# Another order of the second layer's W_in slices in a hybrid decoder trunk

## The chip, the cores and the metric

The kernel runs on one core of a Trainium2 chip. The metric is the device time of one execution in microseconds, lower is better; three runs are given by their median. Engines are named as in the profile: PE is TensorE (matmul; PEld its weight loads), DVE is VectorE, ACT is ScalarE, POOL is GpSimd, SP is the queue that issues the DMAs.

## The reference, cut to what matters

Two layers, 512 tokens, width 1024. One projection W_in feeds three mixers, whose outputs go through W_out; an MLP follows.

```python
for l in range(DEPTH):                                  # DEPTH = 2
    h = _rmsnorm(x, norm_mix_g[l])
    z = h @ w_in[l]
    q, k, v, qi, ki, wi, u5, z_ssd, xbc, dt_raw = _split(z, IN_SIZES)
    attn_out = _dsa_mixer(q, k, v, qi, ki, wi, ...)     # index scores, top-k of 128 keys, softmax, P x V
    s5_out = _s5_mixer(u5, ...)                         # complex state scan, gelu, gate
    ssd_out = _ssd_mixer(z_ssd, xbc, dt_raw, ...)       # conv, chunked scan, gate by z_ssd
    x = x + concatenate([attn_out, s5_out, ssd_out]) @ w_out[l]
    x = x + (relu(_rmsnorm(x, norm_mlp_g[l]) @ w_up[l]) ** 2) @ w_down[l]
```

In `_dsa_mixer` each query scores all earlier keys with 8 small index heads (`qi`, `ki`, `wi`); the 128 best keys alone take part in its attention.

## The kernel before

Products are in float32, each as three passes on high and low parts: `mm3` (L454 to L460) issues xh x whi, xl x whi and xh x wlo. x lies transposed (channels by tokens, 8 tiles), and a slice of W_in is taken in slabs of 128 or 256 rows. For the second layer the slabs were split earlier and lie in DRAM; `Slabs.load` (L167) fetches high and low parts, five buffers deep, in the order of the slices.

The slices of W_in (`W_SL`): `kv` (keys, index keys, values, index weights, dt), `qi` (index queries), `q` (queries), `xa` and `xb` (the two halves of the SSD inputs), `u5` (S5 input), `z` (the SSD gate). `trunk_in` goes through them in the order of `w_order`. kv, qi and q give token tiles (ACT copies them out of PSUM, L1219 to L1224); xa, xb, u5 and z give channel tiles (DVE multiplies them with the row factors `rb`: L1210, L1202, L1213). u5 goes through DRAM to a layout by channel group (L1205, L1207).

`mixers` runs nine generators side by side: `trunk_in`, `keys` (key rope and transposes, then the index scores of query blocks 1 to 3, L1071 to L1076), `select` (top-k: 16 rounds of MAX, L1086, and MATCH_REPLACE, L1087, for each block; the mask, L1090), `attention` (for the query blocks 0 to 3: split of the queries hhl, L1043, transposes, scores lg, softmax pe, pT, po, ml, L1133), `recurrent` for S5 and for SSD, and three of `out_proj`. `merge` takes the next step of the generator whose clock is lowest; the clocks advance by estimated costs times the `pace` of the plan, and `prio` shifts priorities. A scheduler then fixes each engine's order by these priorities, by what is ready and by buffers. PSUM has two groups of four banks, m and a; `bank` in the plan says which tile uses which (qi, q, xb, u5, z: m; xa, scores: a).

S5 (`s5`): s5v products from u5 (L709), ACT copies (L713 to L715), rotation and scan on DVE (L724 to L736, result X), s5y on PE (L748, L749), transposes (L760), gelu over DVE and ACT (`ge`, L762 to L766), glu products (L775), gate (`sig`, L777, L779), then high part `mh` on ACT (L784) and low part `ml` on DVE (L785). SSD (`ssd`): softplus of dt in 25 rows of 128x16 (L803 to L825, L332 to L352), conv (L844 to L858), four chunks (L869 to L920).

Of the kernel before, what the change touches and what calls it, by code (L numbers as in the profile page):

```python
# [69 lines left out]
        "bank": {"w_kv": "m", "w_qi": "m", "w_q": "m", "w_u5": "m", "w_xa": "a", "w_xb": "m", "w_z": "m", "kT": "a", "hT": "a", "ix": "a", "lg": "a", "pT": "m", "po": "a", "sB": "m", "sst": "a", "sU": "a", "sv": "m", "sy": "m", "st": "m", "sg": "a", "dds": "a", "dseg": "m", "darow": "m", "dT": "a", "ds": "a", "dy": "a", "dst": "a", "dn": "a", "db": "m"},  # L70
    },
    {
        "w_order": ("kv", "xa", "qi", "z", "u5", "q", "xb"),
        "top": ((1,), (2,), (3,)),
        "out": (("s5",), ("att",), ("ssd",)),
        "serial": "no",
# [1505 lines left out]
```

## Time and profile before

| | us |
|---|---|
| median of three runs | 1332.54 |
| the runs | 1331.55 to 1332.56 |
| the profiled execution, its own time | 1328.87 |
| its span | 1327.1 |
| PE busy | 1218.0 (92%) |
| DVE busy | 885.2 (67%) |
| ACT busy | 549.2 (41%) |

The mixers of the second layer lie between about 710 and 936 us of the span; ahead of them is the first layer, behind them the second layer's MLP, in both of which PE is nearly always busy. A busy PE is not a PE at its peak, since its records overlap and its clock has two levels, 1.2 and 2.4 GHz; PEclk is the part of the higher one that was granted.

### The profile page before, as it was taken

What the parts mean: (1) busy time and instruction counts of PE and PEld (TensorE: products, weight loads), DVE (VectorE), ACT (ScalarE), POOL (GpSimd) and SP (SyncE); (2) the same over time, 40 slices, a digit from 0 to 9 for tenths busy, and PEclk for the clock granted to TensorE, in tenths of its full rate; (3) what the DMA queues carried; (4) which work ended last, traced back from release to release, by engine and by line L of the source; (5) the groups of instructions that cost most, each with busy time, mean ns of one, the idle gap of its engine ahead of it and who ended that gap; (6) DMA issues with size and microseconds to landing.
All of it is one profiled execution on the core that took longest, in us unless ns stands there. A gap on an engine that the chain in (4) does not pass through costs nothing.

```text
span 1327.1 us, 17056 instructions
## 1 busy us (share of the span) xinstructions
PE 1218.0 (92%) x5708; PEld 977.1 (74%) x5708; DVE 885.2 (67%) x2024; ACT 549.2 (41%) x1128; POOL 169.7 (13%) x302
## 2 busy tenths in 40 slices
PE   5678957889999989999999989968999999999998
PEld 5566745458888868888888767754788888888887
DVE  5998999857886545665564699975475445444443
ACT  4245444664543533534443234455254233242331
POOL 2385100000796040000000000000000000000000
PEclk9889988899999999999999989978999999999999
DMA  5132220002567647677644634300323333333332
GB/s 189 40 88 70 74 74 24 9 1 72 148 213 257 214 146 252 224 262 230 227 149 137 219 120 124 120 17 1 111 88 97 101 97 96 96 96 99 100 110 81
DMA packets 139688, 161.64 MB, mean 122 GB/s; under 512 B 18768, under 2 KB 107600, under 8 KB 139600
## 3 DMA queue, kind: packets, MB, share of 16 engines
q1 hardware_dynamic: 139600, 160.55, 38.5%
q8 instruction: 45, 0.74, 0.2%
q14 instruction: 43, 0.35, 0.1%
HBM read 128.29 MB, written 31.03 MB: 120 GB/s over the span
## 4 chain that ended last, share of the span: by engine, by line
PE 62%; DVE 19%; issue 7%; POOL 6%; ACT 4%; DMA 1%; SPq 0%; ACTq 0%; DVEq 0%; POOLq 0%
PE pm L458 18%; PE pm L460 18%; PE pm L459 18%; PE po L1128 3%; DVE isc L1087 2%; DVE mx L1086 2%; DVE isc L1076 2%; PE pTp L1123 1%; DVE pe L1107 1%; DVE wlo L192 1%; DMA wraw<-in_w_in_dram 1%; POOL pt L660 1%; DVE cv L847 1%; ACT pe L1108 1%; POOL pt L661 1%
## 5 line engine op out<-in xcount | busy, mean ns | idle before, releaser
L192 DVE TENSOR_TENSOR wlo<-wraw,whi 128x512 fp32r<-128x512 f32 (+1 forms) x312 | 223.2, 718 | 243.0 <-ACT whi L191 241.4
L191 ACT ACTIVATE whi<-wraw 128x512 fp32r<-128x512 f32 (+1 forms) x312 | 194.1, 625 | 374.5 <-PE pm L459 236.9
L458 PE MATMUL pm<-xh,whi 128*128 128x512 f32 x640 | 252.4, 395 | 3.8 <-ACT q L1224 3.2
L460 PE MATMUL pm<-xh,wlo 128*128 128x512 f32 x640 | 250.1, 392 | 1.2 <-DVE wlo L192 1.2
L459 PE MATMUL pm<-xl,whi 128*128 128x512 f32 x640 | 250.9, 392 | 0.0
L460 PE MATMUL pm<-uh,wlo 128*128 128x512 f32 x512 | 199.7, 390 | 0.3 <-DVE wlo L192 0.3
L458 PE MATMUL pm<-uh,whi 128*128 128x512 f32 x512 | 199.6, 390 | 0.0
L459 PE MATMUL pm<-ul,whi 128*128 128x512 f32 x512 | 199.6, 390 | 0.0
L458 PEld LDWEIGHTS pm<-xh,whi 128*128 128x128 f32 x640 | 120.8, 189 | 30.8 <-ACT q L1224 3.9
L460 PEld LDWEIGHTS pm<-xh,wlo 128*128 128x128 f32 x640 | 120.6, 189 | 27.4 <-DVE wlo L192 2.0
L459 PEld LDWEIGHTS pm<-xl,whi 128*128 128x128 f32 x640 | 121.1, 189 | 24.2 <-issue 0.2
L460 PEld LDWEIGHTS pm<-uh,wlo 128*128 128x128 f32 x512 | 96.2, 188 | 20.8 <-DVE wlo L192 0.9
L459 PEld LDWEIGHTS pm<-ul,whi 128*128 128x128 f32 x512 | 96.3, 188 | 20.4 <-issue 0.4
L458 PEld LDWEIGHTS pm<-uh,whi 128*128 128x128 f32 x512 | 96.2, 188 | 20.3 <-issue 0.4
L458 PE MATMUL pm<-whi,xh 128*128 128x512 f32 (+1 forms) x176 | 67.4, 385 | 14.0 <-ACT xh L392 12.8
L460 PE MATMUL pm<-whi,xl 128*128 128x512 f32 (+1 forms) x176 | 66.6, 380 | 1.3 <-DVE xl L394 1.3
L459 PE MATMUL pm<-wlo,xh 128*128 128x512 f32 (+1 forms) x176 | 67.0, 381 | 0.5 <-DVE wlo L192 0.3
L1408 DVE TENSOR_TENSOR ul<-ur,uh 128x512 fp32r<-128x512 f32 x64 | 48.5, 758 | 21.0 <-ACT uh L1407 21.0
L1406 DVE SCALAR_TENSOR_TENSOR ur<-pm,ur 128x512 f32<-128x512 f32 x64 | 43.9, 686 | 23.0 <-ACT ur L1403 22.7
L1414 DVE TENSOR_TENSOR sq<-pm,r2b 128x512 f32<-128x512 f32 x64 | 44.1, 689 | 17.5 <-PE pm L460 17.5
L1407 ACT ACTIVATE uh<-ur 128x512 fp32r<-128x512 f32 x64 | 39.9, 624 | 30.7 <-DVE ur L1406 30.7
L1087 DVE MATCH_REPLACE8 isc<-mx,isc 128x256 f32<-128x256 f32 (+2 forms) x96 | 51.6, 541 | 0.0
(345 smaller groups left out, 1931.4 us busy)
## 6 DMA issues: line engine op xcount, KB each, us to landing
wraw<-in_w_up_dram SPq DMA_DIRECT2D x128, 256.0 KB, 2.8
wraw<-in_w_down_dram SPq DMA_DIRECT2D x128, 256.0 KB, 2.8
st<-shi SPq DMA_DIRECT2D x48, 256.0 KB, 2.9
st<-slo SPq DMA_DIRECT2D x48, 256.0 KB, 3.5
wlo<-st SPq DMA_DIRECT2D x48, 256.0 KB, 3.0
whi<-st SPq DMA_DIRECT2D x48, 256.0 KB, 2.8
wraw<-in_w_in_dram SPq DMA_DIRECT2D x32, 256.0 KB, 2.8
sraw<-in_w_in_dram SPq DMA_DIRECT2D x32, 256.0 KB, 3.9
```

The lines of the kernel that those rows point to most:

```text
L191: nc.scalar.activation(hi, raw, AF.Copy)
L192: nc.vector.tensor_tensor(lo, raw, hi.bitcast(F32), ALU.subtract)
L458: nc.tensor.matmul(p, lh, rh, start=first, stop=False)
L459: nc.tensor.matmul(p, lh, rl, start=False, stop=False)
L460: nc.tensor.matmul(p, ll, rh, start=False, stop=last)
L1076: v.scalar_tensor_tensor(acc, r, wi[:, h:h + 1], acc, ALU.mult, ALU.add)
L1087: v.match_replace(acc, m8, acc, SENT)
L1128: nc.tensor.matmul(po[g_ * 64:g_ * 64 + 64], self.vt[:, kb, g_], pts[g_], start=kb == 0, stop=kb == b)
L1406: v.scalar_tensor_tensor(r, p, 0.0, r, ALU.max, ALU.mult)
L1407: nc.scalar.activation(h, r, AF.Copy)
L1408: v.tensor_tensor(lo, r, h.bitcast(F32), ALU.subtract)
L1414: v.tensor_tensor(t, d[1], rb, ALU.mult)
```

## The change

One line of the plan of the second layer: the order of the W_in slices.

```diff
 PLAN = (
...
     {
-        "w_order": ("kv", "xa", "qi", "z", "u5", "q", "xb"),
+        "w_order": ("kv", "qi", "q", "xa", "xb", "u5", "z"),
         "top": ((1,), (2,), (3,)),
         "out": (("s5",), ("att",), ("ssd",)),
```

The line sets the order of the slabs on SP and of the products on PE, and through `merge` and the scheduler the places of all that depends on them. Three places of the DVE queue show it.

The first is right behind the key work of the second layer (klo: low part of the keys; xa, scr, cv: SSD input, softplus and conv; qi, rsw: index queries and their rope; isc: index scores). Before:

```order
L1026 TENSOR_TENSOR klo_7429<-ksb_7148,khi_7427 128x384
L1210 TENSOR_TENSOR xa_7497<-pm_7321,rb_7490 128x512
L344 TENSOR_SCALAR scr_7506<-spe_7502 128x16
L1210 TENSOR_TENSOR xa_7555<-pm_7441,rb_7490 128x512
L345 TENSOR_SCALAR scr_7506<-scr_7506 128x16
L844 TENSOR_SCALAR cv_7635<-xa_7497,hconvw,hconvb 128x512
L346 TENSOR_SCALAR scr_7506<-scr_7506 128x16
L847 SCALAR_TENSOR_TENSOR cv_7635<-xa_7497,hconvw,cv_7635 128x511
```

The change:

```order
L1026 TENSOR_TENSOR klo_7426<-ksb_7148,khi_7424 128x384
L1002 TENSOR_TENSOR rsw_7533<-qi_7531,cols 128x8x8
L1003 TENSOR_TENSOR rsw_7533<-qi_7531,cols 128x8x8
L1004 TENSOR_TENSOR qi_7531<-qi_7531,cols 128x8x16
L1005 TENSOR_TENSOR qi_7531<-qi_7531,rsw_7533 128x8x16
L1043 TENSOR_TENSOR hhl_7538<-qi_7531,hhl_7538 128x4x64
L1043 TENSOR_TENSOR hhl_7548<-qi_7531,hhl_7548 128x4x64
L1073 TENSOR_SCALAR isc_7558<-irl_7562,wd_7150 128x256
```

The two xa tiles, the softplus and the conv behind the keys are gone from here; the index queries follow at once.

The second is S5 from its last X to its last ml (mx and isc: top-k; ge, sig, ml: S5). Before, from ge on:

```order
L764 TENSOR_TENSOR ge_8231<-ge_8231,s5yT_8226 128x512
L1087 MATCH_REPLACE isc_7773<-mx_2429_8988,isc_7773 128x384
L766 SCALAR_TENSOR_TENSOR ge_8220<-ge_8220,s5yT_8215 128x512
L766 SCALAR_TENSOR_TENSOR ge_8231<-ge_8231,s5yT_8226 128x512
L1086 MAX mx_2430_8991<-isc_7773 128x8
L1087 MATCH_REPLACE isc_7853<-mx_2500_9237,isc_7853 128x512
L1087 MATCH_REPLACE isc_7773<-mx_2430_8991,isc_7773 128x384
L1086 MAX mx_2501_9240<-isc_7853 128x8
L1086 MAX mx_2434_9011<-isc_7773 128x8
L779 SCALAR_TENSOR_TENSOR sig_8244<-sig_8244,ge_8220 128x256
L779 SCALAR_TENSOR_TENSOR sig_8244<-sig_8244,ge_8231 128x256
L1087 MATCH_REPLACE isc_7773<-mx_2434_9011,isc_7773 128x384
```

The change, from X on:

```order
L735 TENSOR_TENSOR sws_8613<-sws_8613,SIN_4941 128x512
L736 TENSOR_TENSOR X_2343_8580<-sw_8604,sws_8613 128x8x63
L763 TENSOR_SCALAR ge_8664<-ge_8664 128x512
L764 TENSOR_TENSOR ge_8664<-ge_8664,s5yT_8659 128x512
L763 TENSOR_SCALAR ge_8675<-ge_8675 128x512
L764 TENSOR_TENSOR ge_8675<-ge_8675,s5yT_8670 128x512
L766 SCALAR_TENSOR_TENSOR ge_8664<-ge_8664,s5yT_8659 128x512
L766 SCALAR_TENSOR_TENSOR ge_8675<-ge_8675,s5yT_8670 128x512
L779 SCALAR_TENSOR_TENSOR sig_8688<-sig_8688,ge_8664 128x256
L779 SCALAR_TENSOR_TENSOR sig_8688<-sig_8688,ge_8675 128x256
L785 SCALAR_TENSOR_TENSOR ml_8693<-sig_8688,mh_8692 128x512
```

Before, top-k rows of blocks 2 and 3 (isc 128x384 and 128x512) stand between S5's rows; now the last top-k row stands ahead of S5 and S5's rows follow each other.

The third is the first split of query block 2, hhl (gm, dec, xd, yss: SSD chunk 0; x: out products of S5 added to x; CT, cv: conv; z: the gate). Before:

```order
L844 TENSOR_SCALAR cv_8864<-xb_8862,hconvw,hconvb 128x512
L847 SCALAR_TENSOR_TENSOR cv_8864<-xb_8862,hconvw,cv_8864 128x511
L847 SCALAR_TENSOR_TENSOR cv_8864<-xb_8862,hconvw,cv_8864 128x510
L847 SCALAR_TENSOR_TENSOR cv_8864<-xb_8862,hconvw,cv_8864 128x509
L857 MEMSET CT_8871 64x512
L857 MEMSET CT_8872 64x512
L858 SCALAR_TENSOR_TENSOR CT_8871<-cth_8869,cv_8864 64x512
L1043 TENSOR_TENSOR hhl_8909<-q_8414,hhl_8909 128x4x64
L858 SCALAR_TENSOR_TENSOR CT_8872<-cth_8869,cv_8864 64x512
L894 TENSOR_TENSOR gm_8938<-ssds_8939,cons 128x256
L1043 TENSOR_TENSOR hhl_8919<-q_8414,hhl_8919 128x4x64
L896 TENSOR_TENSOR dec_8890<-dec_8890,gm_8938 128x512
```

The change:

```order
L1213 SCALAR_TENSOR_TENSOR z_8875<-pm_8722,rb_8172 128x512
L1133 TENSOR_TENSOR ml_7936<-po_8439,mh_7932 128x128
L1373 TENSOR_TENSOR x_103<-x_103,pm_8821 128x512
L1133 TENSOR_TENSOR ml_7937<-po_8439,mh_7933 128x128
L1373 TENSOR_TENSOR x_107<-x_107,pm_8833 128x512
L1133 TENSOR_TENSOR ml_7938<-po_8439,mh_7934 128x128
L1373 TENSOR_TENSOR x_113<-x_113,pm_8841 128x512
L1373 TENSOR_TENSOR x_117<-x_117,pm_8853 128x512
L894 TENSOR_TENSOR gm_8938<-ssds_8939,cons 128x256
L1043 TENSOR_TENSOR hhl_8909<-q_7892,hhl_8909 128x4x64
L896 TENSOR_TENSOR dec_8890<-dec_8890,gm_8938 128x512
L1043 TENSOR_TENSOR hhl_8919<-q_7892,hhl_8919 128x4x64
```

Before, the split follows the conv of xb; now the adds of S5's out products and z's tiles stand ahead of it. Behind it the rows are the same but for one add of x.

## Rows read from the trace of the kernel before

**Rows 1.** The page's slices: busy tenths of PE and DVE in 40 equal parts of the span.

```profile
PE   5678957889999989999999989968999999999998
...
DVE  5998999857886545665564699975475445444443
```

**Rows 2.** Stage windows: from:to, us; busy us of each engine (instructions); PEclk; DMA share, GB/s.

```profile
712.00:880.40 168.40, 145.98 (x728) 114.42 (x726) 140.72 (x446) 68.83 (x179) 0.53 (x1) 0.94 0.39 125
790.00:840.00 50.00, 44.34 (x241) 36.44 (x242) 49.78 (x151) 20.66 (x45) 0.53 (x1) 0.90 0.43 130
```

**Rows 3.** Timeline of DVE: start, us, engine, line, operation, output<-inputs, [idle before <-releaser].

```profile
733.05 0.69 DVE L1210 TENSOR_TENSOR xa<-pm,rb 128x512 f32<-128x512 f32 x1 [6.71 <-ACT rb L1192]
...
747.49 0.23 DVE L1002 TENSOR_TENSOR rsw<-qi,cols 128x64 f32<-128x64 f32 x1 [4.35 <-ACT qi L1224]
```

**Rows 4.** Timeline of PE behind the key slices: first xa, first qi, first key transpose.

```profile
710.97 0.39 PE L458 MATMUL pm<-xh,whi 128*128 128x512 f32 x1
...
716.43 0.39 PE L458 MATMUL pm<-whi,xh 128*128 128x512 f32 x1
...
721.51 0.90 PE L1030 MATMUL kTp<-cons,khi 128*128 128x128 f32 x3 [2.88 <-ACT khi L1024]
```

**Rows 5.** Timeline of ACT: first PSUM block of kv emptied, first index queries copied.

```profile
712.69 0.27 ACT L1221 ACTIVATE wd<-pm,rstd 128x12 f32<-128x12 f32 x1
...
746.77 0.69 ACT L1224 ACTIVATE qi<-pm,rstd 128x512 f32<-128x512 f32 x1 [3.05 <-PE pm L460]
```

**Rows 6.** Timeline of DVE ahead of the last attention blocks; 880.38 is block 2's first split.

```profile
851.98 0.29 DVE L1133 TENSOR_TENSOR ml<-po,mh 128x128 fp32r<-128x128 f32 x1 [0.71 <-ACT mh L1132]
...
872.26 0.29 DVE L1133 TENSOR_TENSOR ml<-po,mh 128x128 fp32r<-128x128 f32 x1 [2.91 <-ACT mh L1132]
...
872.47 0.74 DVE L847 SCALAR_TENSOR_TENSOR cv<-xb,hconvw,cv 128x510 f32<-128x510 f32 x1
...
880.38 0.42 DVE L1043 TENSOR_TENSOR hhl<-q,hhl 128x256 fp32r<-128x256 f32 x1
```

**Rows 7.** Timeline of DVE: a small chain alone, and a small row between others.

```profile
740.61 1.23 DVE L816 SCALAR_TENSOR_TENSOR spq<-spq,sps 128x16 f32<-128x16 f32 x6
...
837.02 0.17 DVE L326 SCALAR_TENSOR_TENSOR rst<-rst,qms 128x32 f32<-128x32 f32 x1
...
837.12 0.41 DVE L1043 TENSOR_TENSOR hhl<-q,hhl 128x256 fp32r<-128x256 f32 x1
```

**Rows 8.** Timelines of DVE, PE and ACT: u5, s5v, then pT and po of block 0.

```profile
785.97 1.12 DVE L1202 TENSOR_TENSOR u<-pm,rb 128x512 f32<-128x512 f32 x1
...
792.26 3.76 PE L709 MATMUL s5v<-U,BPT 128*128 128x128 f32 x16 [5.24 <-DVE isc L1087]
...
849.74 0.60 ACT L1125 ACTIVATE pT<-pTp 128x512 f32<-128x512 f32 x1 [1.98 <-PE pTp L1123]
...
850.56 1.07 PE L1128 MATMUL po<-pT,vt 128*64 128x512 f32 x2
```

**Rows 9.** Timeline of DVE: S5 from its last X to its first ml.

```profile
811.10 0.66 DVE L736 TENSOR_TENSOR X<-sw,sws 128x504 f32<-128x504 f32 x1
...
817.24 0.90 DVE L763 TENSOR_SCALAR ge<-ge 128x512 f32<-128x512 f32 x2
...
818.05 1.28 DVE L764 TENSOR_TENSOR ge<-ge,s5yT 128x512 f32<-128x512 f32 x2
...
819.78 1.27 DVE L766 SCALAR_TENSOR_TENSOR ge<-ge,s5yT 128x512 f32<-128x512 f32 x2
...
823.68 0.74 DVE L779 SCALAR_TENSOR_TENSOR sig<-sig,ge 128x256 f32<-128x256 f32 x2
...
825.69 1.08 DVE L785 SCALAR_TENSOR_TENSOR ml<-sig,mh 128x512 fp32r<-128x512 f32 x1
```

**Rows 10.** Windows of PE's granted clock behind waits; columns as in rows 2.

```profile
792.00:796.00 4.00, 3.73 (x17) 3.54 (x17) 4.00 (x12) 1.14 (x3) 0.53 (x1) 0.50 0.59 170
...
884.00:888.00 4.00, 4.00 (x20) 3.38 (x19) 1.95 (x6) 2.29 (x7) 0.00 (x0) 0.50 0.00 0
```

## The prediction

> **What bounds the kernel now.** I read the page's slices first: behind the opening, VectorE (DVE) has its only stretch of nines a little past the middle of the span, and just there TensorE (PE) has its one dip, 9968 [rows 1]. The stage windows say why [rows 2]: from 712 us, when the second layer's row factors are ready, to 880.4 us, DVE is busy 140.72 of 168.40 us, and from 790 to 840 it is busy 49.78 of 50. PE is busy 145.98 of the same 168.40, but in part it waits inside this for DVE. So this stage ends when DVE has got through its queue, and since an engine takes its queue in order, the stage costs the DVE work plus the DVE waits. The work is the same in both kernels (same formulas, same shapes). I forecast the change in the waits.
>
> I measure at one instruction, **E**: the first split (L1043) of query block 2, at 880.38 [rows 6]. From E on both kernels have nearly the same rows on PE, DVE and ACT (blocks 2 and 3 of the attention, the SSD chunks), so a later E is a later end. 168.40 - 140.72 = 27.7 us before E is not busy on DVE; the waits that follow are parts of it.
>
> **The change part by part.** The table moves the slices; PLAN's paces stay. No instruction is added or dropped; what moves are W_in's slabs (their loads on SP too), the products on them and all that hangs on these.
>
> (a) *Index queries first.* Now PE does 48 products for xa from 710.97 on, and DVE waits 6.71 us for ACT's rb and 4.35 us for the first index queries [rows 3]; ACT's copy of the first of them, from 746.77, lets DVE go [rows 5]. One product takes (716.43 - 710.97) / 24 = 0.2275 us. Without xa's 48 products (10.9 us), the rb broadcast and the stop at sds, that copy comes some 15 us sooner, at about 731. The banks cost nothing net: qi needs PSUM bank m, which ACT empties from 712.96 on [rows 5], so PE stands still for 2 us, but it stood still for 2.88 us at 721.51 in any case, for khi [rows 4]. DVE reaches its first index row at about 732 instead of 747.49. But the 10 us of xa, conv and softplus work that it did meanwhile are only put off. What counts is the wait: 11.06 us of it become 5.8 (from 733.05 - 6.71 = 726.3, the end of the key work, to 732). **-5.5** (bounds -4 and -6.5).
>
> (b) The waits of 2.91 and 0.71 us for ACT's copies of attention output [rows 6], and three of 0.15 to 0.29 beside them for out products, lose their place: **-4.3**.
>
> (c) The softplus chain of SSD (some 25 rows of 128x16) stood alone, 6 rows in 1.23 us, 0.205 each; a small row that stands between independent ones takes the queue for 0.10 (837.02 to 837.12) [rows 7]. In the new order the chain alternates with top-k and conv rows: about 25 x 0.1, **-2.4** (bounds 0 and -3). The Trainium skill's page Perfetto Trace Analysis (section Per-instruction lifecycle) says that each DVE instruction pays a fixed bubble for its memory latency; with that alone the order would not matter and this term would be 0. The rows show otherwise, and I take the rows.
>
> (d) The first attention block comes before xa on PE. Its second PSUM result reaches DVE about 1.4 us late instead of 0.7: **+0.7**, within the bounds of (e).
>
> (e) *The last three heads of index block 3.* Their scores now stand on PE between products for xa, behind the transpose of query block 1, which waits for DVE's split. From that split to the eighth head: 30 products (6.8 us), three score pairs and a transpose (1.8), ACT's relu (0.7), 9.3 us. DVE has twelve top-k and mask rows of about half a microsecond to do meanwhile, 6.2 us, so it waits 3.1. PE has just stood still for 2 to 3 us there, and after such stops the rows show 1.2 GHz: granted clock 0.50 in 792 to 796, behind a wait of 5.24 us [rows 8, 10]. Nine or ten of the 30 products at twice 0.2275 add 2.2: **+5** (bounds 2 and 8). Only behind this can top-k of block 3 begin.
>
> (f) *S5's input.* u5 is now taken off PSUM late, and from there to the first s5v it was 5.2 us (787.09 to 792.26, through DRAM on SP) [rows 8]. This trip lies beside top-k rows and block 1 of the attention. But the fourth s5v stands on PE behind block 1's P x V, which needs rows that DVE normalises last. From these rows on: pT 0.6 and po 1.07 [rows 8], s5v 0.9 (a quarter of 3.76), ACT's six small copies, for which I put 2, and 1 us of hand-overs, against some 2 us of DVE work: **+3.5** (bounds 1 and 5).
>
> (g) *The cover of S5 is gone.* This is the largest term. Before, S5's DVE rows stood among top-k rows of blocks 2 and 3, and its hops over PE and ACT were filled. In the new order top-k is finished (its last row stands just ahead of the first sv), and DVE has from sv to ml nothing but S5; what follows stands behind it in the queue. Each hop becomes a DVE wait, of the length that the trace shows [rows 9]: last X ends at 811.76, first ge row at 817.24: 5.5 (s5y, two copies, transposes, square). ge to ge over ACT's tanh: I put 0.6 (it was 0.45, with a top-k row in it: 819.33 to 819.78). Last ge row ends at 821.05, sig at 823.68: 2.6 (glu, tanh). sig's end at 824.42 to ml at 825.69: 1.2 (mh on ACT), twice. Sum **+11.1** (bounds 9 and 12.5). In the trace of before none of these shows as a wait of DVE: the windows have it busy 49.78 of 50 us there [rows 2].
>
> (h) *The out products of S5* then stand between ml and E on PE: 48 products, 10.9 us, with po, arow, ssdT and ssds among them; z's two tiles and two more share bank m, so x2 to x6 also wait for DVE adds. From ml's end to E I count 13.7 us, DVE's own rows there 12.0: **+1.7** (bounds 0 and 3).
>
> (i) *Clock.* During the hops of (g) PE stands still for 2 to 5 us at a time. By the granted clock of 0.50 after such stops [rows 10], I give s5y +1.7, glu +1.8 and the out products +1.5: **+5** (bounds 1 and 9).
>
> (j) *Behind E.* Before, PE came to E out of a nearly idle stretch and had granted clock 0.50 until 888 [rows 10]; now it comes out of the out products. **-1.5** (bounds 0 and -3).
>
> Sum: -5.5 - 4.3 - 2.4 + 0.7 + 5 + 3.5 + 11.1 + 1.7 + 5 - 1.5 = **+13.3**; walked through in order of time, engine by engine with the same durations, so that PE's stops pile up, I come to +16. I take the middle, +14.5. The profiled execution took 1328.87 with a span of 1327.1; its span becomes 1341.6. The median of the runs is 3.7 above that execution, so I add to the median: 1332.5 + 14.5 = **1347.0**, 1.1% more. All bounds low give -3, all high +30.
>
> **Rivals.**
>
> *The filled engine (faster).* DVE stays full from the first index row to E, as it does from 790 to 840 now [rows 2]: its rows start some 15 us sooner, the last waits go, and S5 finds something to run beside. Then only (a) to (c) count: 1332.5 - 12.2 = 1320.3. For it: top-k is the long chain, and it does start sooner. Against it: nothing stands beside S5 in the DVE queue, and an engine that waits at the head of its queue doesn't go past, as in the 2.91 us with conv rows (872.47 the first) ready behind it [rows 6]. It decides if S5's hops cost under 2 us in all. Chance 0.08. The Trainium skill's Perfetto Trace Analysis (section Engine Utilization) says that in a well-optimized kernel at least one engine should come near full use; read as a rule for this stage, it is this rival, and the rows from 790 to 840 fit it, while the new order doesn't.
>
> *PE early (no change).* (e), (f), (h) and (i) come to nothing, because PE keeps 2.4 GHz and waits less: -12.2 + 0.7 + 11.1 - 1.5 = -1.9, 1330.6. Against it: PE waits for DVE's splits in (e) whatever its clock. Chance 0.08.
>
> *PE slow (slower still).* PE's stops keep it at 1.2 GHz through S5 and the whole out block: 48 products at 0.43 (about twice 0.2275) instead of 0.2275 add 10 us to (h), of which (i) has 1.5. 1347 + 8.5 = 1355.5, with (e) at its upper end 1358.5. For it: granted clock 0.50 as late as 884 to 888, behind a stretch in which PE was nearly idle [rows 10]. Chance 0.15.
>
> **How the numbers follow.** Forecast (1337 to 1353): 0.69; PE slow 0.15; no change 0.08; filled engine 0.08. Range 1337 to 1358: it leaves out the two rivals below and the end of the one above. A measurement of this kernel can't tell less than 0.2% (2.7 us) from no change; slower by more 0.84, within 0.08, faster by more 0.08.
>
> **What the profile of the changed kernel would show.** DVE's first L1002 on qi near 732. Waits on DVE before the last two L1076 of block 3 (2 to 3 us each). L763 with a wait of 5 to 7 us for ACT's ge, L779 with 2.5 to 4.5 for ACT's sig, both L785 with about 1.2 for mh. E at 893 to 899 rather than 880.38. In this stretch PE with granted clock 0.5 to 0.8. I am wrong if these waits are there but E isn't later (then DVE work shrank), or if they are short (then S5's hops were not what the rows of before show), or if E is later by this and the end is not (then the tail had slack).

## The result, and the profile after

The changed kernel takes **1350.84 us** (median of four runs, 1347.38 to 1353.67) against 1332.05 for the kernel before in the same comparison: a ratio of 1.0146, 95% interval 1.0132 to 1.016, or 18.8 us more. The forecast was 1347.0 with a range of 1337 to 1358.

The profiled execution of the changed kernel took 1353.67 us with a span of 1351.9, 24.8 more than the span before. 3.6 us of that arise ahead of the second layer's mixers, in code that is the same in both: the row factors' first DVE row (L420) starts at 713.28 instead of 709.68. In the profiles of the twelve experiments below it starts between 710.9 and 714.2, so it is the profiled execution of before that was early. I therefore measure from this row, **M**, to E. M to E was 880.38 - 709.68 = 170.7 us, and is 904.68 - 713.28 = 191.4: **+20.7**. From E to the span's end it was 446.7 and is 447.2. The profiled execution of the changed kernel is the slowest of its four, which is one reason why 20.7 is more than 18.8.

The page's slices of the changed kernel; they answer to [rows 1]:

```profile
PE   5778967889999989999999887787999999999998
...
DVE  5998999757787535565654979576475444445443
```

The one dip of PE (9968) has become six slices (887787), and DVE has lost its run of nines. Stage windows of the changed kernel, columns as in [rows 2]:

```profile
715.60:904.70 189.10, 155.67 (x733) 120.88 (x733) 142.31 (x447) 69.41 (x179) 0.53 (x1) 0.91 0.34 108
...
867.00:877.00 10.00, 6.39 (x54) 6.06 (x55) 1.97 (x3) 2.34 (x6) 0.00 (x0) 0.55 0.01 4
...
881.00:887.00 6.00, 5.86 (x15) 4.78 (x16) 1.49 (x4) 1.29 (x3) 0.00 (x0) 0.56 0.00 0
888.00:900.00 12.00, 9.92 (x40) 6.08 (x39) 10.45 (x18) 3.44 (x7) 0.00 (x0) 1.00 0.27 87
```

The stage is 20.7 us longer, DVE's busy time 142.3 instead of 140.7: the loss is waiting. The two stretches in the middle lie in S5's hops, the times in which S5's chain is on PE and ACT and DVE has to wait for it: DVE and ACT are mostly idle there, and PE has little more than half its clock (granted 0.55 and 0.56). The waits, from DVE's timeline of the changed kernel (start, us, engine, line, operation, tiles, [idle before <-releaser]):

```profile
736.11 0.23 DVE L1002 TENSOR_TENSOR rsw<-qi,cols 128x64 f32<-128x64 f32 x1 [7.10 <-ACT qi L1224]
...
792.13 0.29 DVE L1133 TENSOR_TENSOR ml<-po,mh 128x128 fp32r<-128x128 f32 x1 [1.72 <-ACT mh L1132]
...
804.48 0.75 DVE L1076 SCALAR_TENSOR_TENSOR isc<-irl,wd,isc 128x512 f32<-128x512 f32 x1 [1.26 <-ACT irl L1071]
807.66 0.75 DVE L1076 SCALAR_TENSOR_TENSOR isc<-irl,wd,isc 128x512 f32<-128x512 f32 x1 [2.42 <-ACT irl L1071]
...
856.82 0.69 DVE L724 TENSOR_TENSOR sv<-sv,COS 128x512 f32<-128x512 f32 x1 [3.63 <-ACT sv L713]
...
868.07 0.69 DVE L734 TENSOR_TENSOR sw<-sw,COS 128x512 f32<-128x512 f32 x1 [1.39 <-ACT sws L733]
...
878.10 0.43 DVE L763 TENSOR_SCALAR ge<-ge 128x512 f32<-128x512 f32 x1 [8.02 <-ACT ge L762]
...
885.65 0.76 DVE L779 SCALAR_TENSOR_TENSOR sig<-sig,ge 128x256 f32<-128x256 f32 x2 [3.82 <-ACT sig L777]
887.63 1.06 DVE L785 SCALAR_TENSOR_TENSOR ml<-sig,mh 128x512 fp32r<-128x512 f32 x1 [1.22 <-ACT mh L784]
...
890.58 1.06 DVE L785 SCALAR_TENSOR_TENSOR ml<-sig,mh 128x512 fp32r<-128x512 f32 x1 [1.22 <-ACT mh L784]
...
904.68 0.43 DVE L1043 TENSOR_TENSOR hhl<-q,hhl 128x256 fp32r<-128x256 f32 x1
```

S5's four waits alone are 8.02 + 3.82 + 1.22 + 1.22 = 14.28 us where [rows 9] show none. The last row is E.

**One sum for all kernels.** For each kernel of the table I add up the brackets of DVE's timeline between M and E ("waits") and call the rest of that stretch the rows' own time; of this the top-k rows (L1086, L1087), each counted from its start to the next row's start (less that row's bracket), stand apart. "Same" counts, in DVE's order, top-k rows that stand right behind a row of their own block, of 96.

| kernel | M to E | waits | rows | top-k | same | median less before |
|---|---|---|---|---|---|---|
| before | 170.7 | 24.8 | 145.9 | 49.2 | 11 | 0 |
| changed | 191.4 | 44.0 | 147.4 | 52.4 | 33 | +18.8 |
| e1 index queries first | 179.9 | 31.1 | 148.8 | 53.0 | 40 | +8.3 |
| e2 u5 last | 187.5 | 40.2 | 147.3 | 50.2 | 18 | +16.7 |
| e3 changed, longer hops | 198.3 | 50.8 | 147.5 | 52.4 | 33 | +25.8 |
| e4 before, longer hops | 176.3 | 30.0 | 146.3 | 49.3 | 15 | +4.9 |
| e5 changed, PE kept busy | 193.4 | 46.0 | 147.4 | 52.4 | 33 | +20.8 |
| e6 changed, s5y by halves | 187.2 | 39.8 | 147.4 | 52.3 | 33 | +18.7 |
| e7 before, s5y by halves | 172.9 | 27.1 | 145.8 | 49.6 | 15 | +1.6 |
| e8 q, then u5 | 180.4 | 30.3 | 150.1 | 54.1 | 44 | +10.7 |
| e9 q early, S5 covered | 172.7 | 26.0 | 146.7 | 50.0 | 20 | -0.2 |
| e10 u5 in front | 185.5 | 42.9 | 142.6 | (some behind E) | 10 | +14.1 |
| e11 top-k of 2 and 3 as one | 171.0 | 25.6 | 145.5 | 49.4 | 9 | +2.9 |
| e12 xb early | 169.1 | 22.8 | 146.3 | 49.5 | 15 | -1.3 |

M to E less 170.7 gives the difference of the medians to within 2.2 us in every row but e11, where it is 2.6: 20.7 for 18.8, 9.2 for 8.3, 16.8 for 16.7, 2.0 for -0.2. The medians come from other executions than the profile, and part of the agreement is luck: the profile of e1 is the fastest of its five executions and needs 442.0 us behind E instead of 446.7, and that of e6 is the fastest of its four.

### The profile page after: what moved, and what is told of

Its sections match the earlier page's. It is cut to its first block, busy times and chain, and to the rows that moved or that the text cites. A ratio compares the mean times of both kernels' runs of the same rounds, so it can differ in the third digit from the quotient of the medians.

```text
span 1351.9 us, 17050 instructions
## 1 busy us (share of the span) xinstructions
PE 1230.7 (91%) x5708; PEld 983.1 (73%) x5708; DVE 886.5 (66%) x2024; ACT 550.0 (41%) x1128; POOL 170.2 (13%) x302
## 4 chain that ended last, share of the span: by engine, by line
PE 72%; DVE 18%; ACT 4%; issue 2%; DMA 2%; POOL 1%; SPq 0%; ACTq 0%; DVEq 0%
PE pm L458 21%; PE pm L460 21%; PE pm L459 21%; PE po L1128 3%; DVE isc L1087 2%; DVE mx L1086 2%; PE pTp L1123 1%; DVE pe L1107 1%; DVE wlo L192 1%; DMA wraw<-in_w_in_dram 1%; DVE isc L1076 1%; DVE cv L847 1%; ACT pe L1108 1%; PE hTp L1046 1%; PE glu L775 1%
## 5 line engine op out<-in xcount | busy, mean ns | idle before, releaser
L458 PE MATMUL pm<-mh,whi 128*128 128x512 f32 x128 | 51.2, 403 | 1.5 <-DVE x L1373 0.6
```

The lines of the kernel that those rows point to most:

```text
L458: nc.tensor.matmul(p, lh, rh, start=first, stop=False)
```

## The experiments

Two theories stood at the start. **Theory 1:** the loss is S5's hops, which have no other DVE rows between them. **Theory 2:** the loss comes from index queries and queries being moved ahead of xa. The first two runs each make one half of the change.

### Each half alone: e1 and e2

```diff
-        "w_order": ("kv", "xa", "qi", "z", "u5", "q", "xb"),
+        "w_order": ("kv", "qi", "xa", "z", "u5", "q", "xb"),
```

> Order kv, qi, xa, z, u5, q, xb: the index queries go first, as in the changed kernel, but S5's input stays where it was, ahead of the queries, and S5's DVE rows keep top-k rows between them (8 rows between the last X and the first L763, 3 ahead of the first L779). Theory 1 (the loss of the change is S5's hops without cover on DVE): the wait before the first L1002 is about 7 instead of 11 us in all (-4), the waits before L763 and L779 stay under 2 us, top-k loses some interleaving (+2): 1329 to 1333 us. Theory 2 (the loss comes from moving the index queries ahead: the top-k rounds then run one block after the other): 1340 us or more, without a long wait in S5.

```diff
-        "w_order": ("kv", "xa", "qi", "z", "u5", "q", "xb"),
+        "w_order": ("kv", "xa", "qi", "z", "q", "xb", "u5"),
```

> Order kv, xa, qi, z, q, xb, u5: the order of before, with S5's input moved to the end alone; no row stands between S5's rows from the last X to the last ml. Theory 1: S5's hops turn into DVE waits (L763 some 8 us, L779 3.8, L785 1.2 twice, sv 3 to 4), less what the lost waits for mh give back (-3 to -4): 1342 to 1350 us. Theory 2 (the loss comes from index queries and queries ahead of xa): 1330 to 1335 us.

e2 took 1348.62 us (ratio 1.0126, 1.0111 to 1.0141): u5's place alone costs 16.7 us, where the whole change costs 18.8. DVE's timeline of e2:

```profile
879.07 0.43 DVE L763 TENSOR_SCALAR ge<-ge 128x512 f32<-128x512 f32 x1 [6.89 <-ACT ge L762]
...
886.14 0.43 DVE L779 SCALAR_TENSOR_TENSOR sig<-sig,ge 128x256 f32<-128x256 f32 x1 [3.33 <-ACT sig L777]
```

e1 took 1340.21 (1.0055, 1.0036 to 1.0074), 7 us above what theory 1 allowed, without a long wait in S5. That is what theory 2 had named for this order, so for the index queries theory 2's number holds. DVE's timeline of e1:

```profile
736.34 0.23 DVE L1002 TENSOR_TENSOR rsw<-qi,cols 128x64 f32<-128x64 f32 x1 [7.09 <-ACT qi L1224]
...
864.74 0.29 DVE L1133 TENSOR_TENSOR ml<-po,mh 128x128 fp32r<-128x128 f32 x1 [2.87 <-ACT mh L1132]
...
883.48 0.29 DVE L1133 TENSOR_TENSOR ml<-po,mh 128x128 fp32r<-128x128 f32 x1 [2.68 <-ACT mh L1132]
```

The first wait for the index queries is shorter, as expected (7.09 for 11.06). But top-k, which can start sooner, is also finished sooner, ahead of attention block 0 (before, its last rows lie in block 1), and from 844 us to E 13 waits add up to 13.6 us; the top-k rows themselves cost 53.0 instead of 49.2. So theory 1 lacked something: **top-k rows are what fills the other chains' hops, and there is a limited number of them.** The halves don't add up (8.3 + 16.7 > 18.8); I take it that both take the filler from the same place, the end of the stage, but no run shows this by itself.

### Longer hops in both kernels: e3 and e4

The same edit in the changed kernel (e3) and in the kernel before (e4):

```diff
-            nc.scalar.activation(t, p, AF.Square)
+            for _ in range(5 if l == 1 else 1): nc.scalar.activation(t, p, AF.Square)
...
-            nc.scalar.activation(t, p, AF.Tanh, scale=0.25, bias=hbias[:, m:m + 1])
+            for _ in range(5 if l == 1 and m == 0 else 1): nc.scalar.activation(t, p, AF.Tanh, scale=0.25, bias=hbias[:, m:m + 1])
```

> The changed kernel with longer hops: in the second layer ACT writes each of the two squares of S5's gelu five times instead of once, and the first tanh of the gate five times (some 12 more ACT rows of 0.55 us, 6.6 us in the hops; no row of DVE or PE more, the same DVE order). Theory 1: S5's hops set the end: +5 to +6.6 us on the changed kernel, 1356 to 1358. Rival (the hops have slack, the loss lies elsewhere): within 1.5 us of the changed kernel.

> The kernel before with the same longer hops of S5 (12 more ACT rows in the second layer). The scheduler puts 17 rows instead of 10 between the last X and the first L763. Theory 1: the longer hops are filled with top-k rows, no new DVE wait: within 1.5 us of 1332. Rival (S5's length counts wherever it stands): +5 to +6.6, 1337 to 1339.

e3 took 1357.74 (1.0198, 1.0181 to 1.0215), 6.9 above the changed kernel: S5's hops are the path that sets the end there. DVE's timeline of e3, then of e4:

```profile
880.08 0.43 DVE L763 TENSOR_SCALAR ge<-ge 128x512 f32<-128x512 f32 x1 [10.36 <-ACT ge L762]
...
890.23 0.43 DVE L779 SCALAR_TENSOR_TENSOR sig<-sig,ge 128x256 f32<-128x256 f32 x1 [6.42 <-ACT sig L777]
```

```profile
824.04 0.43 DVE L763 TENSOR_SCALAR ge<-ge 128x512 f32<-128x512 f32 x1
...
834.13 0.43 DVE L779 SCALAR_TENSOR_TENSOR sig<-sig,ge 128x256 f32<-128x256 f32 x1
...
861.01 0.29 DVE L1133 TENSOR_TENSOR ml<-po,mh 128x128 fp32r<-128x128 f32 x1 [3.86 <-ACT mh L1132]
```

In e3's profile the two hops grew by 4.94 us (10.36 for 8.02, 6.42 for 3.82), not by all that was added. The added rows take 3.9 and 2.9 us on ACT, but s5y took 4.59 us (869.77 to 874.36) instead of 6.17, and PE's share of the second hop was 0.3 shorter: the granted clock was 0.94 from 872 to 876, where the profile of the changed kernel has 0.50. 3.9 less 1.6 and 2.9 less 0.3 are the 2.3 and 2.6 that the waits show. The other 2.0 of the 6.9 us between M and E lie ahead of S5 (klo waits 1.80 instead of 0.71, the first attention block 0.7 more), where the edit changes nothing.

e4 took 1336.78 (1.0038, 1.0023 to 1.0053), +4.9, against theory 1 and next to the rival's range, though not by the rival's way: S5's rows still wait for nothing. The top-k rows that now fill the longer hops are missing beside attention block 0, where a wait of 0.71 [rows 6] has become 3.86 and smaller ones have appeared. A covered hop is not free; it is paid for with filler, and here 5.2 us came back as waits, nearly all of them further on.

### S5 elsewhere: e8, e9 and e10

```diff
-        "w_order": ("kv", "qi", "q", "xa", "xb", "u5", "z"),
+        "w_order": ("kv", "qi", "q", "u5", "xa", "xb", "z"),
```

> Order kv, qi, q, u5, xa, xb, z: the changed order with S5's input two places earlier, so that S5 stands beside the last top-k rows (6 rows between the last X and the first L763, none in the later hops) and xa, conv and softplus come behind it. Theory 1 and 3: the wait before L763 falls to 3 to 6 us, L779 and L785 stay; what lay beside top-k in the changed kernel (conv, softplus) now stands behind S5, top-k rows stand more alone (44 dependent neighbours instead of 33): 1344 to 1351. Rival (u5's late place alone made the loss): 1335 or less.

```diff
-        "w_order": ("kv", "xa", "qi", "z", "u5", "q", "xb"),
+        "w_order": ("kv", "xa", "qi", "q", "u5", "z", "xb"),
```

> Order kv, xa, qi, q, u5, z, xb: the queries go ahead of S5's input as in the changed kernel, but xa stays first, and S5's DVE rows keep their cover (8 rows between the last X and the first L763, 4 ahead of the first L779, 2 ahead of the first L785). Top-k rows that stand right behind a row of their own block: 20 instead of 11 before and 33 in the changed kernel. Theory 1: no wait in S5's hops over 1 us; top-k costs 1.3 us more than before (9 neighbours at 0.15): 1331 to 1335. Rival (queries ahead of S5's input are themselves the loss): 1340 or more, with waits in attention block 0 or in index block 3.

```diff
-        "w_order": ("kv", "xa", "qi", "z", "u5", "q", "xb"),
+        "w_order": ("kv", "xa", "u5", "qi", "z", "q", "xb"),
```

> Order kv, xa, u5, qi, z, q, xb: S5 runs ahead of the index queries, in the time in which DVE of the kernel before waits 11.06 us for PE and ACT (L1210, L1002). No row stands between S5's rows, so its hops are DVE waits again, 13 to 15 us, but the waits for rb and for the index queries (11) fall away in part, and top-k (10 such neighbours) lasts as filler until the last attention block. Theory 1: waits before E of 25 to 35 us in place of 24.8: 1333 to 1343. Rival (an uncovered S5 costs its hops wherever it stands): 1345 to 1350.

DVE's timelines of e8, e9 and e10 at the same two hops; in e10 also the first sv:

```profile
846.00 0.43 DVE L763 TENSOR_SCALAR ge<-ge 128x512 f32<-128x512 f32 x1 [3.92 <-ACT ge L762]
...
851.77 0.42 DVE L779 SCALAR_TENSOR_TENSOR sig<-sig,ge 128x256 f32<-128x256 f32 x1 [2.04 <-ACT sig L777]
```

```profile
847.78 0.42 DVE L763 TENSOR_SCALAR ge<-ge 128x512 f32<-128x512 f32 x1
...
854.34 0.41 DVE L779 SCALAR_TENSOR_TENSOR sig<-sig,ge 128x256 f32<-128x256 f32 x1
```

```profile
753.88 0.69 DVE L724 TENSOR_TENSOR sv<-sv,COS 128x512 f32<-128x512 f32 x1 [7.40 <-ACT sv L713]
...
772.08 0.43 DVE L763 TENSOR_SCALAR ge<-ge 128x512 f32<-128x512 f32 x1 [5.38 <-ACT ge L762]
...
777.85 0.43 DVE L779 SCALAR_TENSOR_TENSOR sig<-sig,ge 128x256 f32<-128x256 f32 x1 [2.03 <-ACT sig L777]
```

e9 took 1331.59 (0.9999, 0.999 to 1.0008), no different from before: queries ahead of S5's input cost nothing as long as rows stand between S5's. This speaks most clearly for theory 1, and against the half of theory 2 that blames the queries; the index queries keep their place here, so it says nothing of what e1 showed. e8 took 1342.22 (1.0073, 1.0059 to 1.0087), 1.8 below its range: the wait of L763 fell as expected and that of L779, which was to stay, fell too (2.04), the waits of attention block 0 and of index block 3 nearly vanished too, and top-k cost 54.1. e10 took 1345.91 (1.0106, 1.0092 to 1.012): the rival was right. I had expected the uncovered S5 to lie in time that DVE loses anyway; but its wait for rb stayed (7.38 us), and S5's waits, 7.40 for sv among them, came on top.

### The clock: e5

```diff
+ [nc.tensor.matmul(o, U[hf][:, gi], tab["M"][qq][:, j], start=True, stop=True) for _ in range(24 if l and (q, j, hf) == (0, 0, 1) else 0)];
  nc.tensor.matmul(o, U[hf][:, gi], tab["M"][qq][:, j], start=True, stop=False)
...
+ [nc.tensor.matmul(p[:, 0], glw[:, 0, 0:P], ysb[0][:, :, 0:64], start=True, stop=True) for _ in range(12 if l and (m, jh, k) == (0, 0, 0) else 0)];
  nc.tensor.matmul(p[:, jh], glw[:, k, m * P:(m + 1) * P], gg[jh][:, :, k], start=k == 0, stop=k == 1)
```

(Each added list and the product behind it are one line of the kernel.)

> The changed kernel with idle-time products on PE in the second layer's S5: 24 more s5y products (of U and M, which need no X) ahead of the first product that waits for the second X, and 12 more glu-sized products of ysb ahead of the first glu; their results are overwritten. The same DVE order. Question: what of S5's hops is PE's clock. In the changed kernel s5y runs from 870.1 to 876.3 and glu from 881.1 to 887.4, both in stretches of granted clock 0.50. Theory 1 (term (i) of the prediction): PE keeps 2.4 GHz, s5y takes some 3.2 us and glu 3.6, the waits of L763 and L779 fall from 8.02 to about 5.5 and from 3.82 to about 2.6: -3 to -5 us, 1346 to 1348. Rival: the clock falls all the same, or the hops are bound by hand-overs: within 1 us of the changed kernel, or up to 2 us slower where the added products stand in the way.

It took 1352.39 (1.0151, 1.0135 to 1.0166), 1.5 above the changed kernel, within the scatter of the two. Windows of e5, then PE's timeline of the changed kernel and of e5, then DVE's of e5:

```profile
868.00:872.00 4.00, 4.00 (x25) 4.00 (x24) 2.08 (x4) 1.25 (x2) 0.00 (x0) 0.62 0.02 8
872.00:878.00 6.00, 5.53 (x78) 5.29 (x76) 0.00 (x0) 1.14 (x4) 0.00 (x0) 1.00 0.01 3
...
884.00:888.00 4.00, 4.00 (x23) 3.51 (x22) 0.76 (x2) 1.12 (x2) 0.00 (x0) 1.00 0.00 0
```

```profile
870.13 0.47 PE L749 MATMUL s5y<-CA,X 128*64 128x128 f32 x1 [3.60 <-DVE X L736]
...
875.73 0.57 PE L749 MATMUL s5y<-CA,X 128*64 128x128 f32 x2
...
881.14 6.26 PE L775 MATMUL glu<-ge,glw 128*128 128x256 f32 x16 [3.27 <-issue]
```

```profile
867.03 6.85 PE L748 MATMUL s5y<-M,U 128*64 128x128 f32 x46
873.62 0.32 PE L749 MATMUL s5y<-CA,X 128*64 128x128 f32 x1
...
877.10 0.38 PE L749 MATMUL s5y<-CA,X 128*64 128x128 f32 x2
...
884.07 3.62 PE L775 MATMUL glu<-ge,glw 128*128 128x256 f32 x16
```

```profile
879.28 0.43 DVE L763 TENSOR_SCALAR ge<-ge 128x512 f32<-128x512 f32 x1 [7.78 <-ACT ge L762]
...
886.72 0.76 DVE L779 SCALAR_TENSOR_TENSOR sig<-sig,ge 128x256 f32<-128x256 f32 x2 [3.71 <-ACT sig L777]
```

The clock was higher: 1.00 from 872 to 878 and from 884 to 888, where the changed kernel has 0.55 and 0.56 in the two hops. The 16 glu products took 3.62 us instead of 6.26, as in the kernel before (3.62 from 820.67), and s5y 3.86 (873.62 to 877.48) instead of 6.17 (870.13 to 876.30). So the lower clock costs 2.3 us in the first hop; in the second, of the 2.6 us for all glu products, 1.9 lie ahead of the first sig (881.14 to 885.65 against 884.07 to 886.72). How much of the rise the added products made stays open: e3, which has none, also shows 0.94 from 872 to 876, though its glu still took 5.19. And the waits of L763 and L779 hardly fell, 7.78 and 3.71 instead of 8.02 and 3.82. I had added too many products: they held PE until 873.6, 2.1 us after the last X (871.50), and until 884.07 ahead of glu. What the clock gave, the queue took. The Trainium skill's Perfetto Trace Analysis (section Matmul Optimizations) says that matmuls should run back to back in batches, since the engine's power follows its use. The windows agree as far as the clock goes (1.00 against 0.55), and the waits suggest that idle products can pay only if they end when the real ones can start.

### Shorter hops: e6 and e7

The same edit in the changed kernel (e6) and in the kernel before (e7): in the second layer, the s5y products of the first X ahead of those of the second.

```diff
-            for j in range(4):
-                for hf in range(2):
+            for a_, b_ in ((0, 0), (0, 1), (1, 0), (1, 1), (2, 0), (2, 1), (3, 0), (3, 1)):
+                for j, hf in (((a_, b_),) if l == 0 else ((2 * (a_ % 2) + b_, a_ // 2),)):
```

> The changed kernel with the second layer's 16 pairs of s5y products in another order: those of the first X ahead of those of the second, so that half of them run while DVE still makes the second X. Same products, same DVE order. Theory 1 (S5's hops set the end): the hop from the last X to the first L763 loses some 3 us (half of 6.2): 1346.5 to 1348.5. Rival (the hops have slack): 1350 to 1352.

> The kernel before with the same order of s5y products in the second layer. The longer hops cost that kernel 4.9 of 6.6 us although no wait stood in S5: the filled hops used up top-k rows that were missing beside attention block 1. Theory 3 (top-k rows are a stock: a hop, covered or not, costs what the stock lacks behind it): a hop that is 2 to 3 us shorter leaves filler for later: -1 to -2.5 us, 1329.5 to 1331. Theory 1 as first told (covered hops cost nothing): within 0.6 of 1332.

DVE's timelines of e6 and of e7:

```profile
876.09 0.43 DVE L763 TENSOR_SCALAR ge<-ge 128x512 f32<-128x512 f32 x1 [5.12 <-ACT ge L762]
```

```profile
820.65 0.43 DVE L763 TENSOR_SCALAR ge<-ge 128x512 f32<-128x512 f32 x1 [2.31 <-ACT ge L762]
```

In e6 the wait fell by the 2.9 us that were expected, but the median is 1350.21 (1.0134, 1.012 to 1.0148), only 0.6 below the changed kernel. Both kernels' runs scatter over 3.6 to 6.3 us, and the two profiles are the fastest of the four executions of e6 and the slowest of the four of the changed kernel; part of the 2.9 can be the clock, 0.86 from 868 to 876 in e6 and 0.50 in the changed kernel. So this leaves open whether the 3 us arrive. e7 took 1333.15 (1.001, 1.0001 to 1.0018) where a gain was expected: the scheduler, which plans by its own estimates, put 6 rows into the hop instead of 10, and a wait of 2.31 arose that was not there before. It seems to have taken the hop for shorter than it is.

### In search of a faster one: e11 and e12

```diff
-        "top": ((1,), (2,), (3,)),
+        "top": ((1,), (2, 3)),
```

> The kernel before with the top-k of blocks 2 and 3 written as one generator, row by row in turn, in the second layer (W_in order as before): 9 instead of 11 top-k rows right behind a row of their own block; top-k of block 3 ends 26 rows earlier. Theory 1 (DVE rows' own time plus waits): nearly the same, 1330.5 to 1333. If filler late in the stage is what counts: slower by 1 to 3.

```diff
-        "w_order": ("kv", "xa", "qi", "z", "u5", "q", "xb"),
+        "w_order": ("kv", "xa", "qi", "xb", "u5", "q", "z"),
```

> Order kv, xa, qi, xb, u5, q, z: S5 keeps its cover (10, 5 and 2 rows), 15 top-k neighbours, the second half of the SSD inputs ahead of S5 and the gate last. Theory 1: the cover and the top-k rows are those of before within 0.6 us, the rest moves between places that don't wait: 1330 to 1334. Rival (the late gate z or the early xb makes a new wait): 1336 or more.

e11 took 1334.63 (1.0024, 1.0015 to 1.0032), 1.6 above what theory 1 allowed and as much slower as filler late in the stage would make it. But up to E it is like before (171.0); behind E it needs 449.3 instead of 446.7, and why it does stays open. e12 took 1330.45 (0.9992, 0.9983 to 1.0001): the lowest median of all, with the fewest waits, but its interval holds no change. No version here is shown to beat the kernel before.

## Why the prediction was right, and where it was off

Its argument held: the same DVE rows, longer waits, E later and the end later by the same. In its order, between M and E in the two profiles (predicted, then measured):

- **(a)** -5.5: **-4.9**. The first waits of 11.06 became 7.10 (5.8 was forecast), and klo's wait, which the step did not have, fell from 1.63 to 0.71. With M's shift of 3.6 taken off, the first index row stands at 732.5, forecast 732. e1 shows what the step left out: an earlier top-k is also an earlier end of the filler.
- **(b)** -4.3: **-4.6** (the waits of [rows 6], 0.71 and 2.91, and four small ones).
- **(c)** -2.4: the softplus chain fell from 4.8 to 2.1 us, **-2.7**, but the top-k rows rose from 49.2 to 52.4, **+3.2**, which the prediction put at nothing. The rule of [rows 7], that a row costs less among independent ones, was applied to the chain and not to top-k. This is the step that failed. Top-k rows, first of the kernel before, with two blocks in turn, then of the changed kernel, with one block alone:

```profile
795.10 1.14 DVE L1086 MAX8 mx<-isc 128x8 f32<-128x384 f32 x2
...
796.22 0.54 DVE L1087 MATCH_REPLACE8 isc<-mx,isc 128x384 f32<-128x384 f32 x1
...
796.75 0.67 DVE L1087 MATCH_REPLACE8 isc<-mx,isc 128x512 f32<-128x512 f32 x1
797.34 1.14 DVE L1086 MAX8 mx<-isc 128x8 f32<-128x384 f32 x2
```

```profile
798.58 0.56 DVE L1086 MAX8 mx<-isc 128x8 f32<-128x384 f32 x1
...
799.83 0.56 DVE L1086 MAX8 mx<-isc 128x8 f32<-128x384 f32 x1
...
809.96 0.69 DVE L1086 MAX8 mx<-isc 128x8 f32<-128x512 f32 x1
810.69 0.09 DVE L1087 MATCH_VALUE_LOAD isc<-mx,isc 128x8 f32 x1
810.76 0.68 DVE L1087 MATCH_REPLACE8 isc<-mx,isc 128x512 f32<-128x512 f32 x1
811.47 0.69 DVE L1086 MAX8 mx<-isc 128x8 f32<-128x512 f32 x1
```

  Two rounds in turn, of 384 and of 512, take 797.34 - 795.10 = 2.24 us. Alone, the one of 512 takes 1.51 (809.96 to 811.47) and one of 384 takes 1.25 (798.58 to 799.83), 2.76 together. In the table, top-k rises with the number of such neighbours, 49.2 at 11 to 54.1 at 44, about 0.15 us each; from 9 to 15 neighbours it lies between 49.2 and 49.6 in no order. The fixed bubble of each DVE instruction that the Trainium skill tells of (Perfetto Trace Analysis, section Per-instruction lifecycle) would have made both alike; these rows, too, speak for the neighbours.
- **(d)** +0.7: **+2.8** (0.61, 0.45 and 1.72). 0.7 of the difference is a slip of the sum: the step counted from a wait of 0.7, which is block 0's 0.71 [rows 6] and which (b) had already taken off; 1.4 was meant and 1.72 came. Not foreseen: PE waited 3.20 us for a slab of xa, until 773.90; its load had left SP only 3 us earlier, at 770.92:

```profile
773.90 0.77 PE L458 MATMUL pm<-xh,whi 128*128 128x512 f32 x1 [3.20 <-DMA whi<-st]
```

  In e8, where u5 stands in this place, PE waits for no slab there, and only 0.62 of the 2.8 is left. The cause of the late load wasn't tried by itself.
- **(e)** +5: **+3.7** (1.26 and 2.42). PE had 1.00 in this stretch, so the 2.2 us for the clock fell away; the wait itself was forecast as 3.1.
- **(f)** +3.5: **+5.9** (3.63, 0.89 and 1.39). The last, for ACT's exchange of halves (sws), was not in the list of hops.
- **(g)** +11.1 and, of (i), 1.7 and 1.8 for s5y and glu at half the clock, 14.6 together: **+14.3**. The largest term, and near in its parts: 8.02 (forecast 5.5 + 1.7), 3.82 (2.6 + 1.8), 1.22 twice (1.2), and nothing for ge to ge (0.6). e3 shows that it sets the end, e2 and e9 that it is the loss of cover, and e5 that 2.3 and 1.9 us of the first two hops go with the clock.
- **(h)** +1.7 and 1.5 of (i) for the out products: **+1.1**, with granted clock 1.00 from 888 to 900.
- Other small waits +0.8 (cv, psum), other rows' time +1.1. Sum: -4.9 - 4.6 - 2.7 + 3.2 + 2.8 + 3.7 + 5.9 + 14.3 + 1.1 + 0.8 + 1.1 = +20.7.
- **(j)** -1.5 behind E: +0.5 in this profile; with the same order e3, e5 and e6 have -0.9, -2.3 and -2.2.

Forecast were +13.3 as a sum and +16 as a walk; the medians differ by 18.8. Up to E, without (j), the sum was +14.8, and the profiles differ by 20.7, 5.9 more. Too low were above all top-k without its neighbours (3.2), sv and sws in (f) (2.4), the first attention block in (d) (2.1) and the small waits and rows (1.9); too high were (h) with its clock (2.1) and (e) (1.3). So the mechanism was right, but that the number came within 3.8 us of the measured one is in part luck, since these errors offset each other. E stands at 901.1 with M's shift taken off, 2 us behind the end of the 893 to 899 that were forecast.

Of the rivals, the filled engine failed at S5, as argued, but e1 and e4 show a second reason that the prediction did not have: even where S5 is covered, the filler runs out. PE slow did not come: the out products ran at 1.00. PE early had the clock right in (e) and for the out products, but the waits of (e), (f) and (g) came all the same, 3.7, 5.9 and 14.3 us.

## What to carry to other kernels

Before moving a step in a queue, list the rows that stand inside its hops, and ask where they would stand afterwards: rows that fill one chain's hops are missing beside the next, so cover is a stock to be spent where the hops are longest. Count also which rows would become neighbours of the row that they depend on; two equal chains are cheaper in turn than one after the other. And start no chain early for its own sake if it is the one that fills all others.

## What was not expected of the hardware

- The price of a dependent neighbour on DVE: about 0.15 us for each top-k row, on rows of 0.4 to 0.7 us; 3.2 us in the changed kernel. No run changes the neighbours alone.
- With thirty-six products that compute nothing PE's granted clock in S5's hops was 1.00 instead of 0.55 and 0.56, and yet the two waits fell by 0.24 and 0.11 us only.
- The same order has PE at different clocks in different executions. In the first hop the profiles of the changed kernel and of e3 show 0.50 and 0.94 from 872 to 876, with the same products on PE up to there. The four runs of the changed kernel lie 6.3 us apart, and the two shorter ones have a mean granted clock of 0.963 and 0.964, the two longer ones 0.958; the 27 runs of before in the last comparison lie within 3.7 us. The scatter does not follow the length of the stops in S5: e1's five runs lie 6.6 us apart without a long one, e3's four 2.3 with the longest. What sets it stays open.
